# Two-layer decoder trunk on one core: where the attention's full-precision probabilities are kept, and how their low parts are summed

## The chip, the core and the metric

The kernel runs on one core of one Trainium2 chip. The core has a matrix engine (TensorE, in the rows PE, with its weight loads as PEld), a vector engine (VectorE, DVE), an activation engine (ScalarE, ACT), a general engine (GpSimd, POOL) and a queue engine that issues most transfers (SyncE, SP). Matrix products are written to PSUM, which has eight banks of 128 rows by 512 float32 numbers; everything else lies in SBUF. The metric is the device time of one execution in microseconds (us), lower being better.

## The reference

A sequence of 2048 tokens with 1024 features goes through two layers. Layer 0 mixes a gated linear recurrence (4 heads) with trailing averages; layer 1 is an attention of 16 heads of 64 features with a forgetting bias. The change touches layer 1, whose core is, in the reference:

```python
logits = (jnp.einsum('bhqd,bhkd->bhqk', q[:, :, q0:q1], k[:, :, :q1]) * scale
          + cumf[:, :, q0:q1, None] - cumf[:, :, None, :q1])
mask = jnp.arange(q0, q1)[:, None] >= jnp.arange(q1)[None, :]
probs = jax.nn.softmax(jnp.where(mask, logits, -jnp.inf), axis=-1)
outs.append(jnp.einsum('bhqk,bhkd->bhqd', probs, v[:, :, :q1]))
```

So each head needs, for each query, the exponentials of the logits of all earlier keys, their sum over the keys, and their product with the values. All of it is float32, and the kernel keeps near float32 precision by splitting an operand `a` into a rounded part `hi` and the rest `lo = a - hi`, which TensorE multiplies in separate passes.

## The kernel before, in words

The tokens are cut into four segments of 512. A segment goes through both layers before the next one starts, and keys and values of earlier segments are read back from DRAM (`k1d`, `k2d`, `vd`). In the attention of segment s (0 to 3), a head has 4(s+1) blocks of 128 keys; each block meets all 512 queries, except the last four blocks (the segment's own keys), which meet 512, 384, 256 and 128 of them. That makes 64, 128, 192 and 256 blocks for the 16 heads of the four segments, 640 in all, and 16 blocks of each of the three short shapes in each segment.

For a block, `attend` (from L1114) does the following. TensorE forms the scores in a PSUM bank `pst` by two products (with K1 and K2; a third adds the mask in the segment's own blocks). ScalarE takes the exponential twice from that bank: `p` in full precision to SBUF (L1152) and `ph`, rounded, to SBUF (L1154). VectorE forms the rest `pl = p - ph` (helper L178). GpSimd adds `p` to the running sum `la` (L1160, L1162). Two blocks later (`LAG = 2`) TensorE multiplies `ph` with `[v_hi | v_lo]` (128 columns) and `pl` with `v_hi` (64 columns), both into the one bank `pov`. At a head's end ScalarE copies the lower half of `pov` out (L1174), VectorE adds the upper half (L1175), and `la` is split into `lh` and `ll`, from which TensorE later takes the sums over the 128 rows (`pL`).

Beside a head's blocks run the maximum of the next head's scores (`max_pass`: a product into a bank `pmx`, then a VectorE reduction, L1094), the preparation of the head after it (`prep`: four transposes into `pqkT`), and the projections of later heads (`pqk`, `pv`, `pgt`), which are spread between the blocks as fill. Every matmul is recorded at the helper line L39.

PSUM banks are dealt out by pools: 2 for projections (`pj`), 2 for scores (`st`), 1 for the output sums (`o`) and 3 for everything else (`mx`: maxima, transposes, small products). The order of the instructions on each engine is fixed at build time by a scheduler that works from the order in which the program emits them and from when it expects operands and buffers to be free; at run time each engine takes its instructions strictly in that order and waits where an operand is not ready. SBUF scratch tiles (`tmp`) share nine slots.

Of the kernel before, what the change touches and what calls it, by code (L numbers as in the profile page):

```python
# [21 lines left out]
ND = D // P          # blocks of the model's width  # L22
SEG = 512            # tokens that go through both layers together
NSEG = T // SEG
NTB = SEG // P       # token blocks of a segment
NH = 16              # heads of the attention
HD = 64
EPS = 1e-6
# [4 lines left out]
def trunk(ctx, tc, x, cvec, norm_g, ada_c, ada_w, ada_b, ada_bg, lbp, w0, w0o, w1, w1f, w1o,  # L33
# [34 lines left out]
    def ps_misc(name):  # L68
        return ps.tile([P, 512], F32, name=name, tag="mx", bufs=3)
# [7 lines left out]
    def ps_o(name):  # L77
        return ps.tile([P, 512], F32, name=name, tag="o", bufs=1)

    def ps_mx(name):  # L80
        return ps.tile([P, 512], F32, name=name, tag="mx", bufs=3)
# [9 lines left out]
    # mq[q, k]: keys after the query, in the last block; mk[k, q]: the same with keys on the partitions  # L91
# [16 lines left out]
    # ones between zeros: the columns from HD on fill a pair's first head, those from 0 on its second  # L108
# [5 lines left out]
    # masks of the halving levels: right halves of each block, compact, for the chunks of a segment  # L114
# [12 lines left out]
    # 1 / min(t + 1, w) for the first positions  # L127
# [22 lines left out]
    vd = dr.tile([NH, P, T // P, P], F32, name="vd")  # L150
# [5 lines left out]
    def rsqrt_mean(out_t, ss, n, name):  # L156
        """out = 1 / sqrt(ss / n + eps) on a small tile"""
# [12 lines left out]
    def silu_from(out_t, src, t):  # L170
        """out = src * sigmoid(src); src may lie in PSUM, t is scratch"""
        S.activation(t, src, AF.Exp, scale=-1.0)
        S.activation(t, t, AF.Ln, bias=1.0)
        S.activation(t, t, AF.Exp, scale=-1.0)
        V.tensor_tensor(out_t, src, t, op=ALU.mult)
# [5 lines left out]
    class Steps:  # L181
        """a queue of generators, taken a step at a time"""
# [27 lines left out]
    def weave(main, nm, fill, keep=0):  # L210
        """the main stream's steps with the fill's spread evenly among them, but for the last ones to keep"""
# [12 lines left out]
    def both(*l):  # L224
        """generators by turns, a step of each; a number bounds how many steps the one before it takes"""
# [39 lines left out]
    # the last two blocks of the last projection's four tiles, times the gate  # L265
# [39 lines left out]
    def proj_T2(pts, wt, act):  # L305
        """two tiles of 128 features, the second half of the contraction for the first token blocks first"""
# [14 lines left out]
    def proj_T(pt, wt, fo, act):  # L321
        """pt[feature, token] = the weights' 128 columns from fo on; two steps"""
# [8 lines left out]
    def proj_N(pt, wt, act, tb, ds=tuple(range(ND)), first=True, last=True):  # L331
        """pt[token of block tb, 256 columns], all of the contraction or some blocks of it"""
# [14 lines left out]
    def mod_cols(l, b, pm, which, n):  # L347
        """n columns of the shift (which = 0) or the scale (1) from their sums"""
# [8 lines left out]
    # which engine sums a block of the shift's and scale's products over d: PE, Vector, GpSimd  # L357
    WHO = ("GV", "PV", "GV", "PV", "GV", "VV", "VV", "VV")

    def ada_first(half, slots, between):  # L360
        """shift and scale of half of layer 0's features"""
# [51 lines left out]
    def ada_rest(scratch):  # L413
        """layer 0's gate, layer 1's shift and scale: products on the vector engine, sums on PE"""
# [31 lines left out]
    def norm_rows(xr, xt, stat=None):  # L446
        """the rows over their root mean square"""
# [25 lines left out]
    def norm_T(l, xr, tb, act, half, shared=True):  # L473
        """four of the rows' blocks, turned, scaled and shifted, in two parts; xr is overwritten"""
# [63 lines left out]
    def hgrn_v(s, hp):  # L538
        L = seg0[s]
        wt, act = next_w(("a", II[hp])), L["act"]  # L540
        vn = kp.tile([P, NTB, 256], F32, name="vn", tag="vc", bufs=3)
# [8 lines left out]
    def gates(L, key, name, wkey):  # L550
        """silu of 256 columns, features on the partitions"""
# [11 lines left out]
    def hgrn_core(s, h, fill):  # L563
        """a head's recurrence over the segment's four chunks"""
# [3 lines left out]
        # diagonal of the scores  # L568
# [39 lines left out]
        for lv in range(NL):  # L608
# [3 lines left out]
            if lv == NL - 2:  # L612
                # what the state gives
# [35 lines left out]
        # norm over the values, which lie on the partitions  # L649
# [61 lines left out]
    # the order of the input projection's tiles  # L711
# [27 lines left out]
    def pre0_proj(s, v=None):  # L739
        """v: what is left of the first values, whose rows may be ready before the other projections' columns"""  # L740
# [11 lines left out]
    def start():  # L752
        """the first segment's activations beside layer 0's modulation"""
# [16 lines left out]
    def layer0(s, before, rest):  # L770
        """before: what is left of the segment before; it fills the first head's time"""
# [42 lines left out]
    def out_first(s):  # L814
        """the output projection's first columns, but for the last head's part"""
# [7 lines left out]
        # a bank holds one open sum  # L823
        L["py"] = wt, [(ps_pj if tb < 2 else ps_mx)("py")[:, 0:256] for tb in range(NTB)]
# [5 lines left out]
    def out_proj0(s):  # L830
        """the layer's output rows, with the sums of squares of each quarter"""
# [34 lines left out]
    def out_end1(s, wi, py, xt, tb, gt, n=2):  # L866
        """the rows of n token blocks from tb on"""
# [246 lines left out]
    def attend(s, h):  # L1114
# [11 lines left out]
        def values(b, q0, kb, vv, ph, pl):  # L1126
            end = kb == nkb - 1
            if end:
                mm(po[0:HD, q0:], vv[:, b, 0:HD], pl[:, q0:], start=False, stop=False)
# [252 lines left out]
```

## Time and profile before

| What | Value |
|---|---|
| Median of three runs | 3137.76 us (3135.08 to 3143.48) |
| Span of the profiled execution | 3139.8 us |
| Busy: TensorE / VectorE / ScalarE / GpSimd | 2830.8 / 2505.1 / 1780.4 / 1226.5 us |
| Attention stretches of segments 0, 1, 2, 3 | about 300 to 690, 930 to 1390, 1680 to 2190, 2500 to 3110 us |
| GpSimd's additions of `p` to `la` (L1162) | 528, 670.5 us |
| VectorE's `pl = p - ph` (tile `pl`) | 624, 572.5 us |

The profile gives no time of the profiled execution apart from its span, first to last instruction; it lies 2.0 us above the median of the runs shown. A busy share says how long an engine's instructions were in flight; TensorE's are pipelined, so one matmul can start before the record of the last one ends. What bounds a stretch is read from what the engines there waited for.

### The profile page before, as it was taken

How to read it: one execution, taken by the hardware profiler on the slowest of the kernel's cores; microseconds unless marked ns; L12 is line 12 of the kernel's file. 1: busy time of each engine (PE TensorE's matmuls, PEld its weight loads, DVE VectorE, ACT ScalarE, POOL GpSimd, SP SyncE). 2: the span in 40 equal slices, each digit the busy share in tenths (PEclk: the TensorE clock that was granted, in tenths of full speed). 3: DMA queues.
4: the chain of work that ended last, by engine and by line, in shares of the span. 5: the costliest groups of instructions: out<-in, count | busy, mean ns of one | idle time of the engine just before them, and what ended most of it. 6: DMA issues, size and time to landing. Idle time of an engine off the chain costs nothing. (4 is left out here: it accounts for less than half of the span.)

```text
span 3139.8 us, 49278 instructions
## 1 busy us (share of the span) xinstructions
PE 2830.8 (90%) x17020; PEld 2393.2 (76%) x17020; DVE 2505.1 (80%) x4518; ACT 1780.4 (57%) x3679; POOL 1226.5 (39%) x944
## 2 busy tenths in 40 slices
PE   5999899999998888899998888889999988888888
PEld 4788788888787777789897767777988866666666
DVE  8776697875868787875768888898666889898997
ACT  3454566753555566663555665666344566666653
POOL 3221232232123444343214555555311265656564
PEclk9999999999999999999999999999999999999999
DMA  6423453333333333334234333332423322222232
GB/s 241 161 78 108 124 150 100 113 105 101 96 115 99 94 104 98 109 91 122 76 124 121 99 112 105 114 118 90 132 75 106 100 88 90 91 92 90 89 121 66
DMA packets 198906, 337.99 MB, mean 108 GB/s; under 512 B 19768, under 2 KB 67000, under 8 KB 196096
## 3 DMA queue, kind: packets, MB, share of 16 engines
q1 hardware_dynamic: 195264, 320.93, 33.4%
q10 hardware_dynamic: 3392, 13.90, 1.3%
q8 instruction: 135, 2.21, 0.3%
q14 instruction: 115, 0.94, 0.1%
HBM read 285.33 MB, written 49.17 MB: 107 GB/s over the span
## 5 line engine op out<-in xcount | busy, mean ns | idle before, releaser
L178 POOL TENSOR_TENSOR wt<-raw,wt 128x512 fp32r<-128x512 f32 x287 | 431.0, 1509 | 1133.8 <-ACT wt L289 1034.8
L1162 POOL TENSOR_TENSOR la<-la,p 128x512 f32<-128x512 f32 (+3 forms) x528 | 670.5, 1270 | 516.5 <-ACT p L1152 451.2
L178 DVE TENSOR_TENSOR pl<-p,ph 128x512 fp32r<-128x512 f32 (+3 forms) x624 | 572.5, 921 | 49.4 <-ACT ph L1154 45.9
L1152 ACT ACTIVATE p<-pst 128x512 f32<-128x512 f32 (+3 forms) x624 | 333.8, 535 | 232.6 <-PE pst L39 173.3
L39 PE MATMUL pqk<-wt,h 128*128 128x256 f32 x3072 | 449.0, 288 | 5.6 <-DVE Vc L178 1.8
L39 PEld LDWEIGHTS pqk<-wt,h 128*128 128x128 f32 x3072 | 421.3, 195 | 24.1 <-issue 3.0
L39 PE MATMUL pgt<-h,wt 128*128 128x512 f32 x1536 | 422.5, 410 | 0.2
L289 ACT CAST wt<-raw 128x512 fp32r<-128x512 f32 x578 | 338.5, 626 | 81.6 <-PE py L39 37.5
L39 PE MATMUL pv<-wt,h 128*128 128x256 f32 x2304 | 352.8, 298 | 7.7 <-DVE h L178 4.8
L1154 ACT ACTIVATE ph<-pst 128x512 fp32r<-128x512 f32 (+3 forms) x640 | 342.7, 535 | 29.8 <-DVE pl L178 24.2
L39 PEld LDWEIGHTS pv<-wt,h 128*128 128x128 f32 x2304 | 326.2, 202 | 25.9 <-DVE h L178 7.7
L39 PEld LDWEIGHTS pgt<-h,wt 128*128 128x128 f32 x1536 | 294.2, 196 | 63.5 <-issue 2.7
L178 DVE TENSOR_TENSOR wt<-raw,wt 128x512 fp32r<-128x512 f32 x291 | 273.3, 942 | 54.9 <-ACT wt L289 53.8
L1094 DVE TENSOR_REDUCE mxs<-pmx 128x1 f32<-128x512 f32 x384 | 251.5, 682 | 23.5 <-PE pmx L39 22.8
L39 PE MATMUL pov<-pl,Vo 128*64 128x512 f32 x384 | 166.0, 432 | 109.5 <-DVE pl L178 104.3
L39 PE MATMUL py<-wt,o 128*128 128x256 f32 x1536 | 204.6, 289 | 0.0
L39 PE MATMUL py<-wt,mix 128*128 128x256 f32 x1536 | 199.0, 288 | 2.3 <-DVE yt L838 1.4
L39 PEld LDWEIGHTS py<-wt,o 128*128 128x128 f32 x1536 | 195.9, 195 | 4.1 <-issue 1.7
L39 PEld LDWEIGHTS py<-wt,mix 128*128 128x128 f32 x1536 | 187.9, 191 | 11.3 <-issue 6.5
L39 PEld LDWEIGHTS pov<-pl,Vo 128*64 128x64 f32 x384 | 53.1, 138 | 178.3 <-DVE pl L178 172.8
L39 PE MATMUL pov<-ph,Vo 128*128 128x512 f32 x384 | 163.5, 426 | 0.0
L39 PE MATMUL pst<-Q,K2o 68*128 68x512 f32 x384 | 150.7, 411 | 14.1 <-DMA K2o<-k2d 11.2
(378 smaller groups left out, 5329.8 us busy)
## 6 DMA issues: line engine op xcount, KB each, us to landing
raw<-in_w_dram SPq DMA_DIRECT2D x448, 256.0 KB
K2o<-k2d SPq DMA_DIRECT2D x192, 136.0 KB
K1o<-k1d SPq DMA_DIRECT2D x96, 256.0 KB
Vo<-vd SPq DMA_DIRECT2D x96, 256.0 KB
raw<-in_w1o_dram SPq DMA_DIRECT2D x66, 256.0 KB
raw<-in_w0o_dram SPq DMA_DIRECT2D x64, 256.0 KB
ada<-in_ada_w_dram ACTq DMA_DIRECT2D x12, 1024.0 KB
k1d<-K SPq DMA_DIRECT2D x48, 256.0 KB
```

Of the source, the lines that this page charges most:

```text
L39: return nc.tensor.matmul(*a, **k)
L178: (eng or V).tensor_tensor(out_t, full, f(hi), op=ALU.subtract)
L289: S.copy(wt[:, 0, sl, :], raw)
L1094: V.tensor_reduce(mxs[:, i, c:c + 1], pm[:, 0:n], axis=AX.X, op=ALU.max)
L1152: S.activation(p[:, q0:], st[:, q0:], AF.Exp)
L1154: S.activation(ph[:, q0:], st[:, q0:], AF.Exp)
L1162: G.tensor_tensor(la[:, q0:], la[:, q0:], p[:, q0:], op=ALU.add)
```

## The change

1. The rounded exponential `ph` is now taken first, and the full-precision one is written over the scores in their PSUM bank instead of into an SBUF tile `p`. VectorE's subtraction reads that bank and `ph`.
2. GpSimd sums `ph` instead of `p`. (In segment 0 it copies the first `ph` to `la`, where ScalarE used to write `p` there directly.)
3. The sum of the `pl` comes from TensorE: the stored values become `[v_lo | v_hi | 1 | 1]` (130 columns, `VW`), the product with `pl` takes 66 columns (`v_hi` and the ones) and goes to a bank of its own, `pol`. At the head's end VectorE adds row 64 of `pol` to row 0 of `la`, and the rows 0 to 63 to the output.
4. The bank for `pol` is taken from the pool `mx`, which has 2 instead of 3; one of layer 0's open sums uses `pol`'s bank.

```diff
-        return ps.tile([P, 512], F32, name=name, tag="mx", bufs=3)
+        return ps.tile([P, 512], F32, name=name, tag="mx", bufs=2)
...
+    def ps_o2(name):
+        return ps.tile([P, 512], F32, name=name, tag="o2", bufs=1)
...
-        L["py"] = wt, [(ps_pj if tb < 2 else ps_mx)("py")[:, 0:256] for tb in range(NTB)]
+        L["py"] = wt, [(ps_pj, ps_pj, ps_o2, ps_mx)[tb]("py")[:, 0:256] for tb in range(NTB)]
...
-        vcs = [kp.tile([P, NTB, 2, P], F32R, name="Vc", tag="vc", bufs=3) for _ in range(2)]
+        vcs = [kp.tile([P, NTB, 2, VW], F32R, name="Vc", tag="vc", bufs=3) for _ in range(2)]
+        for vc in vcs:
+            G.tensor_copy(vc[:, :, :, P:], one1.unsqueeze(1).unsqueeze(1).to_broadcast([P, NTB, 2, 2]))
...
-            if end:
-                mm(po[0:HD, q0:], vv[:, b, 0:HD], pl[:, q0:], start=False, stop=False)
-            mm(po[:, q0:], vv[:, b, :], ph[:, q0:], start=(kb == 0), stop=end)
-            if not end:
-                mm(po[0:HD, q0:], vv[:, b, 0:HD], pl[:, q0:], start=False, stop=False)
+            mm(po[:, q0:], vv[:, b, 0:P], ph[:, q0:], start=(kb == 0), stop=end)
+            mm(pol[0:HD + 2, q0:], vv[:, b, HD:], pl[:, q0:],
+               start=(kb == 0), stop=end)
...
-                p = la if kb == 0 and s == 0 else tmp("p")
-                S.activation(p[:, q0:], st[:, q0:], AF.Exp)
                 ph = tmp("ph", F32R)
                 S.activation(ph[:, q0:], st[:, q0:], AF.Exp)
+                S.activation(st[:, q0:], st[:, q0:], AF.Exp)
                 pl = tmp("pl", F32R)
-                split_lo(pl[:, q0:], p[:, q0:], ph[:, q0:])
+                split_lo(pl[:, q0:], st[:, q0:], ph[:, q0:])
                 if kb == 0:
-                    first = p
+                    first = f(ph)
+                    if s == 0:
+                        G.tensor_copy(la, first)
                 elif kb == 1 and s > 0:
-                    G.tensor_tensor(la, first, p, op=ALU.add)
+                    G.tensor_tensor(la, first, f(ph), op=ALU.add)
                 else:
-                    G.tensor_tensor(la[:, q0:], la[:, q0:], p[:, q0:], op=ALU.add)
+                    G.tensor_tensor(la[:, q0:], la[:, q0:], f(ph[:, q0:]), op=ALU.add)
...
-        u = L["u", pair][:, 0, :]
-        lo_ = tmp("lo_")
-        S.copy(lo_[0:HD], po[HD:P])
-        V.tensor_tensor(u[j * HD:(j + 1) * HD], po[0:HD], lo_[0:HD], op=ALU.add)
+        u = L["u", pair][j * HD:(j + 1) * HD, 0, :]
+        S.copy(u, po[HD:P])
+        V.tensor_tensor(la[0:1], pol[HD:HD + 1], la[0:1], op=ALU.add)
+        V.tensor_tensor(u, po[0:HD], u, op=ALU.add)
+        V.tensor_tensor(u, pol[0:HD], u, op=ALU.add)
```

The order of instructions moves with it. TensorE in the last segment's attention, before (a row is a line, an instruction, output and inputs with their buffer numbers, the output's shape, the engines waited for, and a count; `pv1` is projection fill, `Vo` the values read back):

```order
L39 MATMUL pst_29951<-Q1_29387,K1o_29905 128x512 [waits Activation_49]
L39 MATMUL pst_29951<-Q3_29388,K2o_29907 128x512
L39 MATMUL pov_29904<-ph_29928,Vo_29909 128x512
L39 MATMUL pov_29904<-pl_29930,Vo_29909 64x512 [waits DVE_49]
L39 MATMUL pv1_29855<-wt_29405,h1_26331 128x256 x5
L39 MATMUL pst_29974<-Q1_29387,K1o_29968 128x512 [waits DMAHW0_49,Activation_49]
```

and with the change:

```order
L40 MATMUL pv1_29756<-wt_29093,h1_26099 128x256 x5
L40 MATMUL pst_29625<-Q1_29075,K1o_29582 128x512 [waits DVE_49]
L40 MATMUL pst_29625<-Q3_29076,K2o_29584 128x512
L40 MATMUL pol_29581<-pl_29605,Vo_29586 66x512
L40 MATMUL pov_29580<-ph_29614,Vo_29586 128x512 [waits Activation_49]
L40 MATMUL pv1_29756<-wt_29093,h1_26099 128x256 x6
```

Before, the scores of a block wait for ScalarE's second exponential of the block two earlier, and the product with `pl` behind them waits for VectorE. With the change the scores themselves wait for VectorE, the product with `pl` follows without a wait of its own, and the product with `ph` has moved ahead by one block.

VectorE at the end of a head in the last segment, before (`mr` belongs to the next head's maximum, `ssq` to a later projection):

```order
L1111 CAST mr<-pmt 8x128 [waits DMAHW4_49,PE_49]
L178 TENSOR_TENSOR pl<-p,ph 128x128 [waits Activation_49]
L1175 TENSOR_TENSOR u<-pov,lo__29809 64x512 [waits Activation_49]
L178 TENSOR_TENSOR ll<-la,lh 128x512 [waits Activation_49]
L1014 TENSOR_REDUCE ssq<-sqk 128x8 [waits Activation_49]
```

and with the change:

```order
L1117 CAST mr<-pmt 8x128 [waits DMAHW4_49,PE_49]
L182 TENSOR_TENSOR pl<-pst,ph 128x128 [waits Activation_49,Pool_49]
L1180 TENSOR_TENSOR la<-pol,la 1x512 [waits PE_49,Pool_49]
L1181 TENSOR_TENSOR u<-pov,u 64x512 [waits Activation_49]
L1182 TENSOR_TENSOR u<-pol,u 64x512 [waits DVE_49]
L182 TENSOR_TENSOR ll<-la,lh 128x512 [waits Activation_49]
```

Two instructions have come between the last `pl` and `ll`; the first of them waits for TensorE's last product into `pol` and for GpSimd's last addition to `la`.

## Rows read from the trace of the kernel before

**Rows 1.** First part of the page: engine, busy us, share of the span, instructions.

```profile
PE 2830.8 (90%) x17020; PEld 2393.2 (76%) x17020; DVE 2505.1 (80%) x4518; ACT 1780.4 (57%) x3679; POOL 1226.5 (39%) x944
```

**Rows 2.** Busy time of each engine in the four attention stretches, with granted clock.

```profile
300.00:690.00 390.00, 362.50 (x2397) 319.58 (x2396) 295.12 (x626) 252.09 (x549) 108.86 (x94) 0.97 0.38 114
930.00:1390.00 460.00, 403.22 (x2330) 337.33 (x2329) 374.54 (x664) 285.34 (x595) 190.68 (x152) 0.94 0.34 102
1680.00:2190.00 510.00, 448.90 (x2409) 356.30 (x2409) 449.04 (x738) 332.03 (x679) 273.06 (x204) 0.97 0.35 107
2500.00:3110.00 610.00, 523.16 (x2719) 403.99 (x2719) 549.97 (x818) 377.06 (x750) 367.21 (x269) 0.96 0.30 92
```

**Rows 3.** TensorE's waits: four stretches in order, then whole span (total, times, longest).

```profile
PE pov L39 <- DVE pl L178: 3.2, 6, 0.8
...
PE pov L39 <- DVE pl L178: 31.1, 27, 3.7
...
PE pov L39 <- DVE pl L178: 33.7, 51, 2.2
...
PE pov L39 <- DVE pl L178: 62.5, 94, 2.9
...
PE pst L39 <- ACT ph L1154: 4.6, 5, 2.5
...
PE pmx L39 <- DVE mxs L1094: 5.9, 11, 0.8
```

**Rows 4.** Views by tile: count, shortest/median/longest ns, first and last start.

```profile
L178 DVE TENSOR_TENSOR pl<-p,ph x624: 268/754/1819, 368.1 to 3118.3; 128x512 fp32r<-128x512 f32 x144, 128x384 fp32r<-128x384 f32 x4, 128x256 fp32r<-128x256 f32 x4, 128x128 fp32r<-128x128 f32 x4
...
L178 DVE TENSOR_TENSOR ll<-la,lh x64: 668/683/695, 375.7 to 3120.7; 128x512 fp32r<-128x512 f32 x64
...
L1196 DVE TENSOR_TENSOR u<-u,sg x32: 678/1766/1781, 403.6 to 3124.0; 128x512 f32<-128x512 f32 x32
...
L175 DVE TENSOR_TENSOR sg<-pgt,sgt x32: 667/678/693, 388.4 to 3015.9; 128x512 f32<-128x512 f32 x32
...
L178 DVE TENSOR_TENSOR Vc<-pv,Vc x64: 406/419/426, 350.2 to 2957.1; 128x256 fp32r<-128x256 f32 x64
...
L1162 POOL TENSOR_TENSOR la<-la,p x528: 452/1292/2035, 368.1 to 3118.3; 128x512 f32<-128x512 f32 x112, 128x384 f32<-128x384 f32 x43, 128x128 f32<-128x128 f32 x11, 128x256 f32<-128x256 f32 x10
```

**Rows 5.** VectorE on the tile pl in the four stretches (PE, PEld, DVE busy).

```profile
300.00:690.00 390.00, 20.32 (x78) 10.34 (x79) 39.80 (x65) 0.97 0.38 114
930.00:1390.00 460.00, 46.75 (x126) 17.22 (x126) 104.76 (x128) 0.94 0.34 102
1680.00:2190.00 510.00, 74.86 (x186) 26.00 (x186) 180.25 (x188) 0.97 0.35 107
2500.00:3110.00 610.00, 103.03 (x250) 34.45 (x250) 249.17 (x249) 0.96 0.30 92
```

**Rows 6.** Groups by shape, whole span: count, busy us, mean ns, idle before and releaser.

```profile
L1152 ACT ACTIVATE p<-pst 128x512 f32<-128x512 f32 x432 | 259.6, 601 | 160.6 <-PE pst L39 129.8 <-POOL la L1162 13.5 <-DVE pl L178 7.9
...
L1154 ACT ACTIVATE ph<-pst 128x512 fp32r<-128x512 f32 x448 | 268.3, 599 | 22.8 <-DVE pl L178 21.4 <-POOL acc L930 1.2
...
L1094 DVE TENSOR_REDUCE mxs<-pmx 128x1 f32<-128x512 f32 x384 | 251.5, 682 | 23.5 <-PE pmx L39 22.8
...
L39 PE MATMUL pst<-Q,K1o 128*128 128x512 f32 x384 | 159.0, 422 | 1.1 <-ACT ph L1154 0.7
...
L39 PE MATMUL pst<-Q,K2o 68*128 68x512 f32 x384 | 150.7, 411 | 14.1 <-DMA K2o<-k2d 11.2 <-DMA Q<-mr 2.7
...
L1096 DVE CUSTOM_DVE_ANT_0 pmx<-pmx,mq 128x384 f32<-128x384 f32 x64 | 36.3, 568 | 5.9 <-PE pmx L39 5.9
```

**Rows 7.** VectorE in order of time, end of a head: start us, us, what, idle before.

```profile
2524.10 0.28 DVE L178 TENSOR_TENSOR pl<-p,ph 128x128 fp32r<-128x128 f32 x1
...
2526.21 0.68 DVE L1175 TENSOR_TENSOR u<-pov,lo__27246 64x512 f32<-64x512 f32 x1 [1.36 <-ACT lo__27246 L1174]
...
2526.82 0.68 DVE L178 TENSOR_TENSOR ll<-la,lh 128x512 fp32r<-128x512 f32 x1
```

More of the change, by code (lines that the diff above doesn't have):

```diff
@@ L27 @@
 HD = 64
+VW = 2 * HD + 2
 EPS = 1e-6
@@ L78, in ps_o @@
         return ps.tile([P, 512], F32, name=name, tag="o", bufs=1)
+    def ps_o2(name):
+        return ps.tile([P, 512], F32, name=name, tag="o2", bufs=1)
     def ps_mx(name):
-        return ps.tile([P, 512], F32, name=name, tag="mx", bufs=3)
+        return ps.tile([P, 512], F32, name=name, tag="mx", bufs=2)
     def f(ap):
@@ L149, in trunk @@
     k2d = dr.tile([NH, HD + 4, T], F32, name="k2d")
-    vd = dr.tile([NH, P, T // P, P], F32, name="vd")
+    vd = dr.tile([NH, P, T // P, VW], F32, name="vd")
     cfd = dr.tile([NH, 4, T], F32, name="cfd")
@@ L540, in hgrn_v @@
         wt, act = next_w(("a", II[hp])), L["act"]
-        vn = kp.tile([P, NTB, 256], F32, name="vn", tag="vc", bufs=3)
+        vn = kp.tile([P, NTB, 2 * VW], F32, name="vn", tag="vc", bufs=3)[:, :, 0:256]
         for t2 in range(NTB // 2):
@@ L1033, in v_quad @@
                 src = v4[:, :, 2 * pj:2 * pj + 2, :]
-                hi = vcs[pj][:, 2 * t2:2 * t2 + 2, :, 0:HD]
+                hi = vcs[pj][:, 2 * t2:2 * t2 + 2, :, HD:P]
                 S.copy(hi, src)
-                split_lo(vcs[pj][:, 2 * t2:2 * t2 + 2, :, HD:P], src, hi)
+                split_lo(vcs[pj][:, 2 * t2:2 * t2 + 2, :, 0:HD], src, hi)
         for pj in range(2):
@@ L1120, in attend @@
         la = kp.tile([P, SEG], F32, name="la", tag="la", bufs=1)
-        po = ps_o("pov")
+        po, pol = ps_o("pov"), ps_o2("pol")
         nkb = NTB * (s + 1)
@@ L1138, in attend @@
                 k2 = old_k2(h, c)
-                vv = kp.tile([P, NTB, P], F32R, name="Vo", tag="vo", bufs=2)
+                vv = kp.tile([P, NTB, VW], F32R, name="Vo", tag="vo", bufs=2)
                 nc.sync.dma_start(f(vv), vd[h, :, c * NTB:(c + 1) * NTB, :])
```

## The prediction

> **What bounds the kernel now.** I read the busy shares first. Over the span TensorE is in flight for 90%, VectorE for 80% [rows 1]; that names TensorE, but it is a mean over unlike stages. So I read the four attention stretches next. TensorE's share there is 93, 88, 88 and 86%, VectorE's 76, 81, 88 and 90% [rows 2]: the longer the list of keys, the more VectorE fills and the less TensorE does. The waits say who holds whom. In the four stretches TensorE stood for 3.2, 31.1, 33.7 and 62.5 us, together 130.5 us, at the product with `pl`, for VectorE [rows 3]. In the last stretch that is 62.5 of the 86.8 us in which TensorE was not busy (610 less 523.16, [rows 2]). VectorE is the bound of the late attention, through one instruction, `pl`.
>
> Why it is slow is in the views by tile [rows 4]. At 512 columns a VectorE subtraction with two SBUF inputs takes 683 ns in the median as `ll`, which runs at a head's end when GpSimd has done its additions. The same shape as `u` times `sg` takes either about 678 or about 1770 ns, and `pl` goes up to 1819 ns. The difference is about one GpSimd addition (median 1292 ns), so it looks as if the two engines take turns at something. Instructions with one input in PSUM never show it: `sg` 667 to 693 ns over 32, the split of the values 406 to 426 ns over 64, the reduction of the maxima 682 ns in the mean [rows 4, 6]. Before, `pl` has both inputs in SBUF while GpSimd adds.
>
> **Part 1, `pl` from PSUM.** Its mean over the stretches is 39.80/65 = 612, 104.76/128 = 818, 180.25/188 = 959 and 249.17/249 = 1001 ns [rows 5]. With one input in PSUM I price 512 columns like `sg` (678), 384 like the masked maximum (568, [rows 6]), 256 like the split of the values (419), 128 like the shortest `pl` (268, [rows 4]). The three short shapes together are 1255 ns, 16 times in each segment: 20.1 us. The new means are then (16 x 0.678 + 20.1)/64 = 483, (80 x 0.678 + 20.1)/128 = 581, (144 x 0.678 + 20.1)/192 = 613 and (208 x 0.678 + 20.1)/256 = 629 ns. The relief by stretch is 65 x 0.129 = 8, 128 x 0.237 = 30, 188 x 0.346 = 65 and 249 x 0.372 = 93 us, in all 196 us of VectorE.
>
> [...]
>
> **Part 2, two more VectorE instructions at a head's end.** Each at the 0.68 us of the addition there now, 64 heads: 64 x 2 x 0.68 = 87 us of work. Not all of it is new time. Before, VectorE stood for 1.36 us between the last `pl` and the addition to `u`, waiting for ScalarE's copy [rows 7]. The addition to `la` needs only TensorE's product, not that copy, so it fits into this gap; the second addition to `u` does not. I take 0.7 us a head, 45 us or 11 per stretch, between 0 (both hidden) and 1.36 (87 us). The new wait, for `pol` and for GpSimd's last addition, has the additions to `u`, `ll` and the next head's first `pl` queued behind it; it is short as long as GpSimd is done before TensorE, as it was before (`ll`, which needs the finished `la`, starts with no wait, [rows 7]). VectorE's net relief: 8 - 11 = -3, 19, 54 and 82 us.
>
> **Part 3, how much of it reaches the end.** TensorE cannot gain more from `pl` than it waited for it. By stretch the smaller of relief and wait is -3, 19, 33.7 and 62.5: 112 us. In stretches 2 and 3 more relief than wait is left, so the order after it is TensorE's own work.
>
> **Part 4, the scores wait for VectorE.** The bank `pst` was free after ScalarE's second exponential and is now held to the end of `pl`. One bank's round, at means: two score products 0.42 + 0.41, two exponentials 0.60 + 0.60, `pl` 0.68 [rows 4, 6]: 2.71 us, or 3.39 with one maximum's reduction ahead of `pl`. Two banks make two blocks of one round, so a block needs 1.4 to 1.7 us. The stretches give it 460/128 = 3.6, 510/192 = 2.7 and 610/256 = 2.4 us, and `pl` stood in the same place for TensorE before, one product with `ph` and two scores later. So the round does not bind in the mean, but in dense places with little fill the waits come back. TensorE's wait for ScalarE at that bank is small now (4.6 us, [rows 3]). I charge 20 us; bounds: 0 and the whole 112. No row shows ScalarE writing to PSUM. The nearest: VectorE's masked maximum, in place in PSUM, and its reduction out of it fit the same line (568 ns for 384, 682 for 512 columns), so I charge nothing, between -0.1 and +0.1 us on 640 exponentials of an engine with 38% to spare in the last stretch. [...]
>
> **Part 5, small things.** A third `mx` bank less: TensorE's waits for the maximum's reduction were 5.9 us [rows 3]; I charge 3 us, between 0 and 20 (some four times that row, as the transposes and `pL` sit in the same pool). TensorE: 66 columns instead of 64 as the matmul's rows, the same 512 columns streamed, 0. GpSimd: 16 copies to `la` at an addition's 1.3 us, 21 us, and 32 small copies of ones at most 0.45 us each (the shortest addition, [rows 4]), 14 us; it is busy 109 of 390 us in the first stretch [rows 2], which hides both. If a ones copy waits for its buffer, additions and weight splits queue behind it, and at a head's end VectorE's `la`. Values through DRAM: 130 instead of 128 columns, 1.6% more on SP's queue for that transfer, nothing. Fewer `tmp` slots are used per block (two, not three), which can only free ScalarE. The last head: the sum to `la` puts one more 0.68 us into the tail; 1 us.
>
> **The sum.** 112 - 20 - 3 - 1 = 88 us off the span of 3139.8: 3051.8. The span lies 2.0 us above the median of the runs, so I predict 3050 us. Own range: the best case is the whole net relief (19 + 54 + 82 = 155 us, 2983 by the median), the worst a relief halved by part 4 (56 - 24 = 32 us, 3106).
>
> **Rivals.**
> - *All of VectorE's relief counts* (15%). Before, VectorE itself set the pace where it is 90% busy, and each us saved is a us gained, as TensorE's stalls also cost the ends of its pipelined matmuls: about 2985 us. For it: 93 us relief against a VectorE idle time of 60 us in the last stretch. Against it: TensorE has 86% there.
> - *The wait only moves* (13%). TensorE's wait at `pl` becomes a wait of the scores for `pl`, nearly as long: 3125 to 3140 us. For it: both wait for the same block's `pl`, and the scores stand ahead of the product (the order of TensorE in the section on the change).
> - *The bank's round binds: slower* (12%). If two instructions come ahead of `pl`, one of them with two SBUF inputs at 1.78 us [rows 4], the round is 2.71 + 0.68 + 1.78 = 5.2 us, 2.6 per block. It decides from 2.4 on, the last stretch's pace: (2.6 - 2.4) x 256 = 51 us more there and no gain elsewhere: about 3190 us. For it: VectorE has 90% of that stretch, and other work does get ahead of `pl`. Against: that work itself becomes rarer to wait for when `pl` is short. [...]
> - *PSUM does not free `pl`* (5%). Then part 1 is nothing, parts 2, 4 and 5 stay: 3139.8 + 45 + 24 - 2 = 3207 us. Against it: the narrow spread of `sg` and the split of the values, made while GpSimd was busy 28 to 60% of each stretch [rows 2].
>
> The forecast itself has 55%. A measurement of this kernel tells no change from one of 0.3%, 9 us. Faster by more than that: 55 + 15 + half of the second rival, less a little: 0.75; within it 0.08; slower 0.17. For 8 in 10 the range reaches from just below the first rival, 2980, to the second's end, 3140.
>
> **What would show it.** `pl` at 128x512 with a median near 680 ns and a longest under 800; VectorE's busy time down by some 110 us (196 less 87). GpSimd's long additions in the last stretch at its median of 1.29 us, not above. TensorE's wait for `pl`, now named at `pst`, between 20 and 60 us in all. Stretch 3 shorter by about 50 us, stretch 2 by 25, stretch 0 not at all. I am wrong if `pl` keeps lengths over 1 us, if `pst` waits for VectorE over 100 us, or if `pmx` waits tens of us for its reductions.

## The result, and the profile after

The changed kernel takes 3058.4 us in the median of four runs (3056.6 to 3062.8); the kernel before took 3140.6 beside it (3135.1 to 3145.8). The ratio is 0.974, with a 95% interval of 0.9726 to 0.9755. The prediction was 3050. Its time was right within 8 us, but several of its terms were not: errors of both signs cancelled, as the experiments show.

Part 1 of the page of the changed kernel (engine, busy us, share, instructions):

```profile
PE 2799.8 (92%) x17020; PEld 2378.7 (78%) x17020; DVE 2373.8 (78%) x4646; ACT 1792.8 (59%) x3679; POOL 1191.7 (39%) x992
```

Against [rows 1], VectorE is busy 131 us less, although it has 128 instructions more. TensorE, with the same 17020 matmuls, is busy 31 us less. The span fell by 82.4 us, to 3057.4, so the other 51 us are less time in which TensorE stood still.

The four attention stretches of the changed kernel, now cut at their first and last score product (window, its length, then busy time of PE, PEld, DVE, ACT and POOL, granted clock, DMA share, GB/s):

```profile
356.00:673.00 317.00, 284.90 (x1839) 245.95 (x1838) 250.12 (x547) 203.33 (x431) 102.29 (x102) 0.98 0.43 114
964.00:1380.00 416.00, 371.16 (x2164) 308.04 (x2163) 334.63 (x664) 273.18 (x565) 173.02 (x151) 0.96 0.40 104
1671.00:2175.00 504.00, 453.88 (x2496) 365.49 (x2494) 415.41 (x790) 342.52 (x696) 265.21 (x215) 0.98 0.41 114
2464.00:3037.00 573.00, 527.24 (x2831) 416.75 (x2829) 485.66 (x884) 385.56 (x764) 340.71 (x278) 0.98 0.33 101
```

and the kernel before, cut in the same way:

```profile
356.00:663.00 307.00, 284.67 (x1836) 247.80 (x1836) 238.51 (x516) 200.54 (x430) 88.19 (x80) 0.97 0.39 114
955.00:1387.00 432.00, 377.89 (x2165) 314.76 (x2164) 352.97 (x632) 270.09 (x566) 182.49 (x146) 0.94 0.34 100
1676.00:2200.00 524.00, 462.90 (x2486) 367.64 (x2484) 460.13 (x759) 338.11 (x693) 281.37 (x209) 0.97 0.35 108
2489.00:3118.00 629.00, 541.31 (x2819) 419.93 (x2818) 566.52 (x852) 383.03 (x763) 371.73 (x273) 0.96 0.29 92
```

The lengths go from 307, 432, 524 and 629 us to 317, 416, 504 and 573: +10, -16, -20 and -56. The first, where little was to be gained, got longer. VectorE's busy time in the last stretch fell by 81 us (566.5 to 485.7) and TensorE's by 14, with the granted clock going from 0.96 to 0.98.

TensorE's waits over the whole span of the changed kernel (total us, times, longest):

```profile
PE pst L40 <- DVE pl L182: 46.1, 61, 3.4
...
PE pst L40 <- DMA Q<-mr: 30.9, 14, 6.3
...
PE pol L40 <- DVE pl L182: 4.8, 11, 1.5
...
PE pmx L40 <- DVE mxs L1100: 2.3, 5, 1.2
```

Two of these waits in the kernel before, over its whole span:

```profile
PE pov L39 <- DVE pl L178: 131.5, 181, 3.7
...
PE pst L39 <- DMA Q<-mr: 5.0, 3, 2.4
```

The wait for `pl` was 131.5 us over the span and is now 46.1 + 4.8 = 50.9, most of it at the scores. What has grown is the wait for `Q`'s last row, which comes by a DMA from `mr`: in the kernel before the scores waited 5.0 us for it, now they wait 30.9 us in 14 places. The maxima's wait for their reductions did not grow (5.9 before [rows 3], 2.3 now).

The tile views that answer to [rows 4] (count, shortest/median/longest ns):

```profile
L182 DVE TENSOR_TENSOR pl<-pst,ph x640: 268/680/694, 370.3 to 3037.3; 128x512 fp32r<-128x512 f32 x160
```

```profile
L1168 POOL TENSOR_TENSOR la<-la,ph x528: 452/1292/2266, 370.8 to 3037.6; 128x512 f32<-128x512 f32 x112, 128x384 f32<-128x384 f32 x43, 128x128 f32<-128x128 f32 x11, 128x256 f32<-128x256 f32 x10
```

```profile
L1203 DVE TENSOR_TENSOR u<-u,sg x32: 673/826/1469, 406.4 to 3043.5; 128x512 f32<-128x512 f32 x32
```

`pl` has a median of 680 ns and never exceeds 694 (before: 754 and 1819). GpSimd's additions keep their median over all shapes of 1292 ns. An instruction that still has two SBUF inputs, `u` times `sg`, still reaches 1469 ns. VectorE on the tile `pl` alone, in the last two stretches of the changed kernel (length, busy, count):

```profile
1671.00:2175.00 504.00, 118.16 (x191) 0.98 0.41 114
2464.00:3037.00 573.00, 161.74 (x255) 0.98 0.33 101
```

The means are 118.16/191 = 619 and 161.74/255 = 634 ns, against 959 and 1001 before [rows 5]. The two exponentials in the view by shape (count, busy us, mean ns, idle before):

```profile
L1157 ACT ACTIVATE ph<-pst 128x512 fp32r<-128x512 f32 x448 | 267.9, 598 | 215.6 <-PE pst L40 211.7 <-POOL la L1168 0.4
L1158 ACT ACTIVATE pst<-pst 128x512 f32<-128x512 f32 x448 | 266.5, 595 | 0.0
```

The one that writes over PSUM takes 595 ns, the one that writes to SBUF 598; before, both wrote to SBUF and took 599 and 601 [rows 6]. Last, the end of a head on VectorE in order of time (start us, us, what, idle before; the second addition to `u` and `ll` follow later), to set beside [rows 7]:

```profile
2535.98 0.29 DVE L182 TENSOR_TENSOR pl<-pst,ph 128x128 fp32r<-128x128 f32 x1 [0.28 <-ACT pst L1158]
2536.73 0.68 DVE L1180 TENSOR_TENSOR la<-pol,la 1x512 f32<-1x512 f32 x1 [0.46 <-PE pol L40]
2537.44 0.68 DVE L1181 TENSOR_TENSOR u<-pov,u 64x512 f32<-64x512 f32 x1
```

The addition to `la` starts after 0.46 us of idleness, which TensorE's last product into `pol` ends. It and the addition to `u` both take 0.68 us, although the first works on a single row.

### The profile page after: what moved, and what is told of

Read it like the earlier page. It is cut to its first block, busy times and chain, and to the rows that moved or that the text cites. A ratio compares the mean times of both kernels' runs of the same rounds, so it can differ in the third digit from the quotient of the medians.

```text
span 3057.4 us, 49147 instructions
## 1 busy us (share of the span) xinstructions
PE 2799.8 (92%) x17020; PEld 2378.7 (78%) x17020; DVE 2373.8 (78%) x4646; ACT 1792.8 (59%) x3679; POOL 1191.7 (39%) x992
## 3 DMA queue, kind: packets, MB, share of 16 engines
q1 hardware_dynamic: 195264, 321.52, 36.3%
## 4 chain that ended last, share of the span: by engine, by line
PE 49%; DVE 16%; DMA 6%; ACT 5%; issue 3%; POOL 0%; SPq 0%; DVEq 0%; ACTq 0%; POOLq 0%
PE py L40 9%; PE pst L40 6%; PE pgt L40 6%; PE pqk L40 6%; PE pv L40 4%; PE pmx L40 3%; DMA K2o<-k2d 3%; PE pov L40 3%; PE pol L40 2%; PE pq L40 2%; DVE pl L182 2%; PE pl L40 2%; PE pf L40 2%; DVE wt L182 2%; DMA Q<-mr 2%
## 5 line engine op out<-in xcount | busy, mean ns | idle before, releaser
L1168 POOL TENSOR_TENSOR la<-la,ph 128x512 f32<-128x512 f32 (+3 forms) x528 | 614.6, 1164 | 445.4 <-ACT ph L1157 396.5
L182 DVE TENSOR_TENSOR pl<-pst,ph 128x512 fp32r<-128x512 f32 (+3 forms) x640 | 385.7, 604 | 123.2 <-ACT pst L1158 111.1
L40 PE MATMUL pqk<-wt,h 128*128 128x256 f32 x3072 | 457.4, 286 | 5.7 <-DVE h L495 2.6
L1158 ACT ACTIVATE pst<-pst 128x512 f32<-128x512 f32 (+3 forms) x640 | 340.1, 531 | 0.0
L182 DVE TENSOR_TENSOR wt<-raw,wt 128x512 fp32r<-128x512 f32 x291 | 264.2, 912 | 54.7 <-ACT wt L293 53.2
L1100 DVE TENSOR_REDUCE mxs<-pmx 128x1 f32<-128x512 f32 x384 | 258.4, 685 | 46.9 <-PE pmx L40 43.4
L40 PE MATMUL pst<-Q,K1o 128*128 128x512 f32 x384 | 161.9, 427 | 18.8 <-DVE pl L182 18.2
L40 PE MATMUL pst<-Q,K 128*128 128x512 f32 (+7 forms) x512 | 131.8, 335 | 37.1 <-DVE pl L182 27.9
```

Source lines behind the costliest of these rows:

```text
L40: return nc.tensor.matmul(*a, **k)
L182: (eng or V).tensor_tensor(out_t, full, f(hi), op=ALU.subtract)
L1100: V.tensor_reduce(mxs[:, i, c:c + 1], pm[:, 0:n], axis=AX.X, op=ALU.max)
L1158: S.activation(st[:, q0:], st[:, q0:], AF.Exp)
L1168: G.tensor_tensor(la[:, q0:], la[:, q0:], f(ph[:, q0:]), op=ALU.add)
```

## The experiments

All ran beside the kernel before, which took 3134.6 to 3141.2 us in the median. Ratios are to it; a ratio's difference of 0.01 is 31 us.

**1. The change with the full-precision exponential back in SBUF.** It tells whether `pl`'s place matters or the rest of the change.

```diff
-                S.activation(st[:, q0:], st[:, q0:], AF.Exp)
+                p = tmp("p")
+                S.activation(p[:, q0:], st[:, q0:], AF.Exp)
...
-                split_lo(pl[:, q0:], st[:, q0:], ph[:, q0:])
+                split_lo(pl[:, q0:], p[:, q0:], ph[:, q0:])
```

> The changed kernel with the full-precision exponential back in an SBUF tile; all else of the change stays (rounded one first, sum of the rounded ones on GpSimd, bank for pol, ones column, two mx banks). Theory A (pl was slow because both its inputs lay in SBUF while GpSimd adds; one input in PSUM frees it): pl at 512 columns goes back from 0.68 to over 1.0 us in the late stretches, VectorE's busy time rises by some 190 us, and the time to 3130 to 3165 us. Rival B (the gain comes from the rest: the order, the product with ph one block ahead, fewer scratch slots): within 15 us of 3058.

3218.4 us, ratio 1.0238 (1.021 to 1.0265): slower than before, by more than expected. `pl` in this kernel, and TensorE's wait for it:

```profile
L182 DVE TENSOR_TENSOR pl<-p,ph x640: 268/693/1817, 368.8 to 3202.7; 128x512 fp32r<-128x512 f32 x160
```

```profile
PE pol L40 <- DVE pl L182: 113.1, 165, 3.0
```

The long `pl` are back, and so is the wait. All of the gain hangs on the PSUM input; without it the rest of the change makes the kernel about 75 us slower than before.

**2. The kernel before without GpSimd's additions** (`la` is set to one instead, so the sums over the keys are left out). `pl` keeps its two SBUF inputs.

```diff
-                p = la if kb == 0 and s == 0 else tmp("p")
+                p = tmp("p")
...
-                if kb == 0:
-                    first = p
-                elif kb == 1 and s > 0:
-                    G.tensor_tensor(la, first, p, op=ALU.add)
-                else:
-                    G.tensor_tensor(la[:, q0:], la[:, q0:], p[:, q0:], op=ALU.add)
+                if kb == 1:
+                    G.memset(la, 1.0)
```

> The kernel before without GpSimd's additions to la (the sums of the probabilities are left out, la is set to one once a head); p stays in SBUF. Theory A: pl has 683 ns at 512 columns like ll, none over 1.8 us unless a weight split runs beside it; TensorE's wait for pl falls from 131 to under 60 us and the time from 3140 to 3020 to 3060 us. Rival B: pl keeps a mean near 0.92 us over all shapes and the time stays within 15 us of 3140.

2910.2 us, ratio 0.9258 (0.9239 to 0.9278), far below the expected range. `pl` at 512 columns in the kernel before, then in this one and in the changed one (count, busy us, mean ns, idle before):

```profile
L178 DVE TENSOR_TENSOR pl<-p,ph 128x512 fp32r<-128x512 f32 x432 | 462.8, 1076 | 31.2 <-ACT ph L1154 28.4 <-POOL wt L178 1.2 <-ACT r_qk L163 0.3
```

```profile
L178 DVE TENSOR_TENSOR pl<-p,ph 128x512 fp32r<-128x512 f32 x448 | 318.1, 713 | 60.8 <-ACT ph L1154 58.1 <-PE pst L39 0.3
```

```profile
L182 DVE TENSOR_TENSOR pl<-pst,ph 128x512 fp32r<-128x512 f32 x448 | 305.9, 685 | 92.9 <-ACT pst L1158 90.3
```

and over all shapes in this one:

```profile
L178 DVE TENSOR_TENSOR pl<-p,ph x640: 269/682/1792, 359.1 to 2881.0; 128x512 fp32r<-128x512 f32 x160
```

Its mean at 512 columns falls from 1076 to 713 ns, and its median over all shapes from 754 to 682, with both inputs in SBUF. So it is GpSimd's additions that stretch it. TensorE's wait for it falls to 13.1 us. The 231 us that the kernel gains are those of everything that the additions held up, not of `pl` alone; the next experiment, with the additions in place, gives 157. `pl` is long where it has two SBUF inputs beside the additions (1076 ns), and short with two SBUF inputs without them (713) and with one input in PSUM beside them (685). Some long ones remain (up to 1792 ns); GpSimd still has 528 us of other work here, most of it weight splits, but which of them met it was not traced.

**3. Part 1 alone**, in the kernel before: `pl` from PSUM and `ph` summed by GpSimd, but the product with `pl` stays in `pov`, the `mx` pool keeps three banks, and the values stay at 128 columns. The sum of the `pl` is left out of the denominators.

```diff
...
-                S.activation(p[:, q0:], st[:, q0:], AF.Exp)
                 ph = tmp("ph", F32R)
                 S.activation(ph[:, q0:], st[:, q0:], AF.Exp)
+                S.activation(st[:, q0:], st[:, q0:], AF.Exp)
...
-                split_lo(pl[:, q0:], p[:, q0:], ph[:, q0:])
+                split_lo(pl[:, q0:], st[:, q0:], ph[:, q0:])
...
```

> The kernel before with part 1 alone: rounded exponential first, the full one in place in PSUM, pl from there, GpSimd sums ph. The sum of pl is left out of the denominators. No bank for pol, no ones, three mx banks, values at 128 columns, no additional VectorE instructions at a head's end. Theory A: as short a pl as in the change, without its additions: 3005 to 3035 us. Rival B (order and pol's bank made the gain): 3100 us or more.

2987.0 us, ratio 0.9501 (0.9481 to 0.952), 157 us below the kernel before and 18 us below the expected range. Its busy line and waits for `pl`:

```profile
PE 2765.5 (93%) x17020; PEld 2367.3 (79%) x17020; DVE 2294.7 (77%) x4518; ACT 1782.2 (60%) x3679; POOL 1166.8 (39%) x960
```

```profile
PE pst L39 <- DVE pl L178: 47.3, 67, 2.8
...
PE pov L39 <- DVE pl L178: 5.6, 12, 1.4
```

Of the 154.6 us between the profiled spans (3139.8 to 2985.2), 65.3 are TensorE's busy time (2830.8 to 2765.5) and 89.3 its idle time. The waits for `pl` fell from 131.5 to 52.9. The granted clock over the span rose from 0.967 to 0.981.

**4. The same with two `mx` banks**, the third given to `ps_o2` for one of layer 0's open sums, as in the change.

```diff
-        return ps.tile([P, 512], F32, name=name, tag="mx", bufs=3)
+        return ps.tile([P, 512], F32, name=name, tag="mx", bufs=2)
...
```

> Part 1 alone (the sum of pl left out of the denominators) with two mx banks instead of three, the eighth bank used by one of layer 0's open sums only, as in the change. The prediction charged the bank 3 us, between 0 and 20: 2987 to 2995 us, TensorE's wait for the maximum's reductions under 10 us. Rival: the bank is what part 1 alone has over the change with 128-column values (27 us): 3005 to 3015 us.

3006.8 us, ratio 0.958 (0.956 to 0.9599): the bank costs 20 us by the medians and 25 by the ratios. TensorE's waits:

```profile
PE pst L39 <- DVE pl L181: 40.6, 59, 2.8
PE pqkT L42 <- DVE qk L1021: 38.0, 24, 3.8
PE pmt L42 <- DVE mhl L1109: 21.1, 23, 1.4
PE pst L39 <- DMA K2o<-k2d: 20.1, 23, 2.2
...
PE pov L39 <- DVE pl L181: 4.3, 7, 1.4
...
PE pmx L39 <- DVE mxs L1097: 2.7, 5, 1.5
```

`pmx` is not where it shows (2.7 us). The same lines with three banks were 34.0 for `pqkT`, 15.6 for `pmt` and 7.7 for `K2o`, so the cost is spread: 4, 5.5 and 12 us more, and 17 us more of TensorE's busy time (2765.5 to 2782.2), while the waits for `pl` are 8 us less.

**5. That bank given to the scores**: three `pst` banks and two `mx`.

```diff
-        return ps.tile([P, 512], F32, name=name, tag="st", bufs=2)
+        return ps.tile([P, 512], F32, name=name, tag="st", bufs=3)
...
```

> Part 1 alone with two mx banks, and the eighth PSUM bank given to the scores (three pst banks instead of two). The sum of pl is left out of the denominators. Theory (the scores' bank, held to the end of pl, costs): the wait of TensorE for pl at pst, 41 us with two score banks, falls below 15 us, and the time falls from 3007 to 2985 to 2997 us. Rival (the wait only moves one step on, to the product with pl in pov): pst<-pl goes, pov<-pl comes to 25 us or more, and the time stays within 6 us of 3007.

3011.6 us, ratio 0.9588 (0.9568 to 0.9608): nothing gained. The waits:

```profile
PE pov L39 <- DVE pl L178: 46.3, 44, 2.9
...
PE pst L39 <- DMA K2o<-k2d: 39.8, 32, 3.2
```

The scores no longer wait for `pl` at all, and the product with `pl` waits 46.3 us, as much as the 40.6 + 4.3 of experiment 4. TensorE waits for `pl` itself, whichever instruction meets it first; holding the bank costs nothing that shows, as the rival expectation said. The `K2o` wait doubled as well (20.1 to 39.8), so that a small gain hidden behind it can't be excluded.

**6. The change with the values at 128 columns through DRAM**, and the ones written beside them by GpSimd after each load.

```diff
-    vd = dr.tile([NH, P, T // P, VW], F32, name="vd")
+    vd = dr.tile([NH, P, T // P, P], F32, name="vd")
...
-                nc.sync.dma_start(f(vv), vd[h, :, c * NTB:(c + 1) * NTB, :])
+                nc.sync.dma_start(f(vv[:, :, 0:P]), vd[h, :, c * NTB:(c + 1) * NTB, :])
+                G.tensor_copy(vv[:, :, P:], one1.unsqueeze(1).to_broadcast([P, NTB, 2]))
```

> The changed kernel with the values stored to DRAM and read back at 128 columns as before (512-byte pieces instead of 520); the ones are written beside them on the chip, by GpSimd, for each tile read back. Theory V (the 520-byte pieces of the stores occupy the DMA engines longer, and the small transfer of the maximum's rows, which the first scores of a stretch need, lands late behind them): TensorE's wait for that transfer falls from 30.9 to 5 to 10 us and the time from 3058 to 3030 to 3045 us. Rival W (the four stores of a quad happen to be issued together just before that transfer, whatever their width): the wait stays over 20 us and the time within 6 us of 3058.

3014.5 us, ratio 0.9593 (0.9571 to 0.9615), 44 us below the change, more than was expected; it leaves nothing out, and is the fastest version here of which that holds. Its wait for `Q`'s row:

```profile
PE pst L40 <- DMA Q<-mr: 4.5, 4, 1.9
```

So the 130 columns, charged at nothing, cost about half of what the change brings. What of them costs it?

**7. Rows of 130 at a pitch of 144 numbers** (576 bytes) in DRAM; loads and stores then move pieces of 520 bytes.

```diff
-    vd = dr.tile([NH, P, T // P, VW], F32, name="vd")
+    vd = dr.tile([NH, P, T // P, 144], F32, name="vd")
...
```

> The changed kernel with 130-column values in DRAM, but each row of 130 starts at a multiple of 144 numbers (576 bytes) there; the pieces keep 520 bytes. Theory P (where a piece begins: 520-byte pieces laid end to end begin at odd places in DRAM): as good as the values at 128 columns, 3010 to 3025 us, TensorE's wait for the maximum's rows 10 us or less, the queue's share of the DMA engines back under 35%. Theory L (the length of a piece, whatever its place): 3050 to 3065 us, the wait near 30 us, share over 36%.

3022.7 us, ratio 0.9639 (0.9618 to 0.9659), with 12.8 us of waits for `Q`'s row: most of the 44 us is back, with pieces of the same length that begin elsewhere. The time is the one expected of the pieces' place; the wait, and the queue's share of the DMA engines (35.7%), came a little above what was said for it.

**8. Only the store changed.** The values lie head by head in SBUF, so that four rows go out as one piece of 2080 bytes; DRAM layout and loads are those of the change.

```diff
-        vcs = [kp.tile([P, NTB, 2, VW], F32R, name="Vc", tag="vc", bufs=3) for _ in range(2)]
+        vcs = [kp.tile([P, 2, NTB, VW], F32R, name="Vc", tag="vc", bufs=3) for _ in range(2)]
...
-                    nc.sync.dma_start(vd[...], f(vcs[pj][:, :, j, :]))
+                    nc.sync.dma_start(vd[...], f(vcs[pj][:, j, :, :]))
```

> The change with the split values laid out head by head in SBUF, so that the store of a head's values writes four rows of 130 numbers as one run of 2080 bytes per partition instead of four pieces of 520 bytes; DRAM layout and loads are as in the change. Everything is computed. Theory (the stores' small pieces, which begin off the even places, are what the 130 columns cost: 44 us between the change, 3058, and values at 128 columns, 3014.5): 3012 to 3025 us, TensorE's wait pst<-DMA Q<-mr below 13 us, q1's share 34 to 35%. Rival (the loads, which read 2080 bytes from places that are no multiple of 64 bytes, cost it): 3050 to 3062 us, Q<-mr near 30 us, q1's share near 36%.

3020.8 us, ratio 0.9628 (0.959 to 0.9665): the store accounts for about 35 of the 44 us. The start of the third attention stretch shows how. In the changed kernel (timeline: start us, us, what):

```profile
1671.39 3.59 SPq L1047 DMA_DIRECT2D vd<-Vc  x4
...
1675.83 0.65 ACTq L1118 DMA_DIRECT2D Q<-mr  x1
...
1685.08 1.22 PE L40 MATMUL pst<-Q,K2o 68*128 68x512 f32 x2 [6.34 <-DMA Q<-mr]
```

and its DMA engines there (last two columns: DMA share, GB/s):

```profile
1672.00:1676.00 4.00, 4.00 (x31) 3.71 (x30) 3.33 (x13) 0.00 (x0) 0.06 (x1) 1.00 0.84 196
1676.00:1680.00 4.00, 2.73 (x18) 2.35 (x18) 3.06 (x5) 0.59 (x1) 0.00 (x0) 1.00 1.23 104
1680.00:1684.00 4.00, 0.00 (x0) 0.00 (x0) 0.00 (x0) 0.00 (x0) 0.00 (x0) 0.87 0.88 138
```

Four stores are issued from 1671.4, the short transfer of `Q`'s row is issued after them, at 1675.8, and the scores that need it start at 1685.1 after 6.34 us of idleness. From 1676 to 1680 the times of the packets add up to more than the DMA engines have (1.23), and they move only 104 GB/s. The same place with the store in one piece:

```profile
1653.46 3.77 SPq L1047 DMA_DIRECT2D vd<-Vc  x4
...
1657.91 0.65 ACTq L1118 DMA_DIRECT2D Q<-mr  x1
...
1662.36 0.73 PE L40 MATMUL pst<-Q,K2o 68*128 68x512 f32 x2 [1.54 <-DMA Q<-mr]
```

```profile
1654.00:1658.00 4.00, 4.00 (x32) 3.71 (x30) 3.32 (x13) 0.00 (x0) 0.13 (x1) 1.00 0.73 252
1658.00:1662.00 4.00, 2.82 (x19) 2.43 (x18) 3.14 (x5) 0.58 (x1) 0.00 (x0) 1.00 0.93 267
```

Now they move 252 and 267 GB/s, weight loads issued behind the stores included, and the wait is 1.54 us. Over the whole span:

```profile
PE pst L40 <- DMA Q<-mr: 7.4, 5, 2.4
```

That is 23.5 of the 34.8 us between the two profiled spans; TensorE's busy time, 7.3 us less (2799.8 to 2792.5), is most of the rest. What remains to experiment 6 (about 10 us: the loads, the ones copies, and a store in one piece instead of four of 512 bytes) is within the intervals and stays open.

**9. Experiment 6 without the additions of `pol` at a head's end** (both are left out: row 64 to `la`, rows 0 to 63 to `u`).

```diff
-        V.tensor_tensor(la[0:1], pol[HD:HD + 1], la[0:1], op=ALU.add)
         V.tensor_tensor(u, po[0:HD], u, op=ALU.add)
-        V.tensor_tensor(u, pol[0:HD], u, op=ALU.add)
```

> The changed kernel with values at 128 columns in DRAM, without the two additional VectorE instructions at a head's end (the product and the sum with pl are formed, but left out of the output). The prediction charged them 0.7 us of VectorE a head, 45 us, of which part reaches the end. If they are the 27 us between this layout and part 1 alone: 2985 to 2998 us. Rival (the bank is): 3008 us or more.

3011.4 us, ratio 0.9601 (0.9585 to 0.9618), no difference from 0.9593, as the rival expectation said. The two instructions are 80 us of VectorE (busy 2373.5 with them, 2293.3 without), and none of it shows in the time. The wait for `pl` at `pst` falls by 8 us (46.6 to 38.8), and the one of `pqkT` for `qk` rises by 6 (31.1 to 37.1).

**10. A pool of four banks for projections and the rest**, in experiment 6, instead of two and two.

```diff
-        return ps.tile([P, 512], F32, name=name, tag="pj", bufs=2)
+        return ps.tile([P, 512], F32, name=name, tag="mx", bufs=4)
...
```

> The change with the values at 128 columns through DRAM (3014.5 us), with the two banks for projections and the two mx banks made one pool of four; everything is computed. Theory (the third mx bank was worth about 20 us because transposes, maxima and small products wait for each other there): sharing gives half or more of it back, 2995 to 3006 us, TensorE's wait pmt<-mhl below 10 us. Rival (projections held open as fill take the banks that the maxima need, or the order changes for the worse): 3012 us or more, waits at pmx or pmt as before or longer.

3318.3 us, ratio 1.0559 (1.0542 to 1.0577): slower by some 300 us than experiment 6. The waits:

```profile
PE pst L40 <- DMA Q<-mr: 45.3, 27, 3.0
PE pst L40 <- DVE pl L182: 38.4, 46, 3.9
```

No single wait makes up the loss, but the one for `Q`'s row is 41 us longer than in experiment 6 (4.5 there), and the maxima now wait 43 us for ScalarE's `Q` and `K`, where they waited some 5: nearer to what the rival expectation said. TensorE is busy 172 us longer with the same matmuls (2958.5 against 2786.8, granted clock 0.921 against 0.981) and idle 144 us longer. The order has changed as well: TensorE's timeline, in which like instructions in a row make one row, has 4330 rows instead of 5119, so like instructions stand in longer runs. How much of the loss that is was not measured.

## Why the prediction was right, and where its terms were not

The terms, as predicted and as the runs give them (differences of ratios times 3140 us, so that a row carries the error of two ratios, about 10 us; each row is the step from one version to the next, so they add up to the whole by themselves):

| Term of the sum | Predicted | Measured | From |
|---|---|---|---|
| `pl` from PSUM, on the path, with the held bank | -112 + 20 = -92 (with part 2) | -157 | experiment 3 |
| `mx` bank | +3 | +25 | 3 to 4 |
| additions at a head's end, `pol`, ones | in the first term, +1 for the tail | +4 | 4 to 6 |
| values of 130 columns through DRAM: loads and the rest | 0 | +11, unresolved | 6 to 8 |
| the same: stores | 0 | +35 | 8 to the change |
| Sum | -88 | -82 | |

That the sum came so close is luck: the first term was 65 us too small a gain, and the three kinds of cost below it were together 71 us too small.

**What bounds the kernel** was read rightly. VectorE's `pl` was the bound of the late attention, and its length came from GpSimd's additions: without them its mean at 512 columns falls from 1076 to 713 ns (experiment 2).

**Part 1** was right within 1%: means of 613 and 629 ns were forecast for the last two stretches, 619 and 634 came. VectorE's relief was forecast as 196 us; in experiment 3 the tile `pl` is 199 us shorter (642.7 to 443.5, which holds a tile of the same name in layer 0), and VectorE as a whole 210 (2505.1 to 2294.7). Undisturbed, `pl` has a median of 682 ns from SBUF (experiment 2) and 680 from PSUM.

**Part 2** had its work right (80 us against 87) and its place wrong: 45 us were taken off the relief, which made 17 us in the sum (without them the smaller of relief and wait adds up to 129, not 112), and experiment 9 finds none of it in the time. Once `pl` is short, VectorE has time to spare (busy 78% of the span, 85% of the last stretch: 485.66 of 573), and part of what TensorE stops waiting for at one place it waits for at the next (8 us less for `pl`, 6 us more for `qk`).

**Part 3** holds the step that failed: "TensorE cannot gain more from `pl` than it waited for it". The bound holds for waiting (89 us of idle time went, against 130.5 waited), but 65 us more came from the matmuls themselves, which got shorter. One reason is the granted clock. Here is a wait for `pl` in the kernel before, with the matmuls ahead of it (start us, us, what, idle before), and TensorE's clock behind it:

```profile
2530.89 0.40 PE L39 MATMUL pst<-Q,K1o 128*128 128x512 f32 x1
2531.12 0.40 PE L39 MATMUL pst<-Q,K2o 68*128 68x512 f32 x1
2531.35 0.39 PE L39 MATMUL pov<-ph,Vo 128*128 128x512 f32 x1
2534.52 0.69 PE L39 MATMUL pov<-pl,Vo 128*64 128x512 f32 x1 [2.78 <-DVE pl L178]
```

```profile
2534.50:2540.80 6.30, 6.25 (x17) 4.50 (x18) 4.83 (x6) 3.20 (x5) 1.10 (x1) 0.52 0.15 45
2540.80:2545.00 4.20, 4.20 (x20) 3.34 (x19) 3.35 (x7) 3.70 (x7) 2.58 (x2) 1.00 0.23 74
```

After standing still for 2.78 us, TensorE had a clock of 0.52 for the next 6.3 us (1.00 in the 3.7 us before it stood; the trace shows two levels, 0.50 and 1.00), and of 1.00 after them; 17 matmuls took the first window and 20 the second, which is a third shorter. Over the span the clock rose from 0.967 to 0.981. The loss against the full clock, one minus that share times the span, goes from 104 to 57 us, so by this estimate from the two spans the clock explains at most about 47 of the 65 us, as much as it would if TensorE had been busy all through the slow stretches. Where the rest comes from no run separates; the first rival's words ("TensorE's stalls also cost the ends of its pipelined matmuls") would fit it: just before the wait above, matmuls of 0.39 to 0.40 us start 0.23 us apart, and the end of the last one is covered by no other. They do not name the clock.

That rival, at 15%, was not simply the better account. Its 2985 us stood for the whole change, with part 2's 45 us taken off; for part 1 alone, each us of the 196 saved being a us gained, it would give 196 us. The bound of part 3 would allow no more than the 130.5 us that were waited. Part 1 alone gained 157, between the two.

**Part 4** charged 20 us for the held bank. The wait appeared where it was said (`pst`, 46.1 us, within the 20 to 60 that were given), but experiment 5 finds no cost in the bank. What is left is TensorE's wait for `pl` itself, met at the scores; the second rival had the place right, and the size wrong, as the wait shrank from 131.5 to 50.9 us. The third rival (a binding bank round) did not come. ScalarE's writing to PSUM was charged at nothing, and nothing showed (595 ns, against 601 to SBUF before); the 0.1 us around that charge rests on no row.

**Part 5** held the two terms that were mis-sized: the `mx` bank at 3 us measured 20 to 25, at the bound given or just above it, and not at `pmx`, whose wait it was taken from, but at `pmt`, `pqkT` and `K2o`; and "1.6% more on SP's queue for that transfer, nothing" measured 44 us. Bytes were the wrong measure of that transfer. Stores in pieces of 520 bytes laid end to end filled 4 us at 104 GB/s, while pieces of 520 bytes at another pitch brought most of the time back (experiment 7, 3022.7 us): length alone does not decide. The 66 columns at 0 held: the products of `pl` with `Vo` took 432 ns in the mean with 64 columns before and take 406 with 66.

The tests named ahead came out so: `pl`'s median and longest, GpSimd's median and the stretches of segments 3 and 2 (-56 against -50, -20 against -25) as said; VectorE's busy time fell by 131 us, against some 110; the stretch of segment 0 grew by 10 us instead of staying, of which the waits for `Q`'s row are about half (2.4 us there before, 7.9 now); `pmx` waited 2.3 us for its reductions, not tens.

## What to carry to other kernels

An instruction on VectorE with two SBUF inputs that runs beside GpSimd is worth moving to one PSUM input where another engine waits for it (`pl` at 512 columns: 1076 ns before, 685 after); that it held a PSUM bank longer cost nothing that showed here (3006.8 us, and 3011.6 with a bank more). Price the relief of a wait by TensorE's idle time and by what the wait costs the matmuls after it, the clock among it (in experiment 3, 89 us of idle time and 65 of matmuls). Look at where the rows of a transfer begin and in what pieces it is cut, not only at its bytes (3058.4 us in the change, 3022.7 with another pitch, 3020.8 with stores in larger pieces), and at which short transfer stands behind it (30.9 us of waits for `Q`'s row, 7.4 with the store in one piece).

## What the runs showed of the hardware

- GpSimd's additions cost this kernel 231 us of 3141 (experiment 2), although GpSimd was busy only 39% of the span [rows 1]. A `pl` beside them had a mean of 1076 ns at 512 columns from SBUF and 685 from PSUM.
- Stores in pieces of 520 bytes laid end to end in DRAM brought the DMA engines down to 104 GB/s for 4 us at one place (196 in the 4 us before); with the same bytes in pieces of 2080 at the same addresses the two windows there show 252 and 267, weight loads included. On SP's queue that is 176832 instead of 195264 packets for the same 321.52 MB (18432 less: 48 stores x 128 partitions x 3), and 34.5 instead of 36.3% of the engines' time.
